# A mixture-of-experts stage: the overfull experts' branch at the end of the first group, the groups of four in second and fifth place, expert numbers read between transfers, and the embedding product in the second group

## The chip, the cores and the metric

The kernel runs on one core of a Trainium2 chip. A core has five engines that run side by side: TensorE (PE, with its weight loads listed as PEld), VectorE (DVE), ScalarE (ACT), GpSimd (POOL) and SyncE (SP), which here only issues transfers. Each engine works through its own list of instructions in order and waits on semaphores for the others. The metric is the device time of one execution in microseconds (us).

## The reference, cut to what matters

Two transformer blocks run one after the other on 512 tokens of width 1024. The first has a mixer and then a mixture of 32 experts; the second has a mixer, a dense feed-forward layer and a gated addition of a per-token embedding. The two pieces that the change touches are these:

```python
# first block: each token takes 2 of 32 experts (one group of 8 is chosen first)
def expert_block(args):
    xb, e = args
    hid = jax.nn.silu(xb @ w_gate[e]) * (xb @ w_up[e])   # 1024 -> 512, twice
    return hid @ w_down[e]                               # 512 -> 1024
y = jnp.sum(y_buf[dest].reshape(T, TOP_K, D) * weights[..., None], axis=1)
x = x + y

# second block, its last line
h = h + gate * (p @ w_ple)          # p: 512 x 256, w_ple: 256 x 1024, not dependent on h
```

All weights are float32. One expert has 3 matrices of 2 MiB, so the 32 experts are 192 MiB, which the kernel reads once.

## The kernel before, in words

The mixer of the first block runs up to about 340 us of the profile. Then comes the stage of the experts, from about 340 to 862 us, and then the second block.

**Sets and groups.** The router's result is counted on the chip, and the experts are sorted by the number of their tokens into 32 positions; the first 4 positions are fixed experts (0 to 3), so that their weights can be loaded before the routing is known. Positions 0 to 15 are taken in pairs (sets 0 to 7, 64 token slots for each expert), positions 16 to 31 in fours (sets 8 to 11, 32 slots for each). A set is thus always 128 token rows. Two sets are a group, and `GROUPS` gives the order of the six groups. For each group `dispatch` gathers the rows of its 256 slots by 64 matmuls of a one-hot matrix with the tokens (L765), and `expert_rows` then does each set: gate and up product (L841), silu and product, transposes (L852), down product (L859), and the weighted scatter back into the tokens by matmuls (L866, L867) that VectorE adds to `x1` (L869). TensorE's time for a set is the same for a pair and for a four, since two or four experts share the array side by side; the weights are 12 MiB for a pair and 24 MiB for a four.

**Transfers.** The weights come in 192 chunks of 1 MiB (L616, SyncE's queue), in the order in which sets use them: per set gate, up and down, each in two halves. `load_chunks` gives a chunk the next free slot. There are 15 slots at first; two of them (13 and 14) are given to other tiles after their first use, so 13 go round. At each half matrix, the slots of the halves before are given back and the next chunks are asked for; on the chip SyncE waits, chunk by chunk, until TensorE has read the chunk that was in the slot. `cap` limits how far the chunks run ahead of set `S_PLE`: to 9 chunks of it. `chunk_ap` makes the address; for positions 4 and up it needs the expert's number, which SyncE reads from the sorted list with `value_load` (L598).

**The embedding product.** `ple_units` multiplies `p` by `w_ple` (split in high and low parts, 8 output tiles of 6 matmuls, L99). It takes 4 slots out of the ring (`lent`): two for its operands, two for its results, and its pieces are put between the pieces of the experts' work by `fill_in`. What is left of it runs in the second block (`for _ in fill[0]: pass`). Each half of the result (1 MiB) is written to DRAM (L1214).

**The branch.** An expert with more tokens than slots needs further passes. `overflow` counts them, every engine reads the count from SBUF (L962), and a branch (L963) jumps over a loop of such passes when there are none, as with these inputs. No instruction is moved across the branch on any engine.

**The order.** The framework's scheduler orders each engine's instructions ahead of time, by its own estimate of when operands are there, and may put a later group's gathering between an earlier set's products where no branch is in between. TensorE then runs that list strictly in order.

Of the kernel before, what the change touches and what calls it, by code (L numbers as in the profile page):

```python
# [2 lines left out]

# [25 lines left out]
def hybrid_moe_block(ctx: ExitStack, tc: tile.TileContext, A, out):  # L29
    nc = tc.nc  # L30
# [16 lines left out]
    def slot(i, dt=F32):  # L47
        if i >= 13:
            return mp.tile([128, 2048], dt, name=f"slot{i}", tag="zz" if i == 13 else "yy", bufs=1)
        if i >= NSLOT:  # L50
            return prt.tile([128, 2048], dt, name=f"slot{i}", tag=f"s{i}", bufs=1)
        return slots.tile([128, 2048 if 6 <= i < 10 else WB], dt, name=f"slot{i}", tag=f"s{i}")
# [5 lines left out]
    def bank(tag, shape=(128, 512)):  # L58
        return psp.tile(list(shape), F32, name=f"ps_{tag}", tag=tag, bufs=NPS[tag])
# [35 lines left out]
    def mm3(ps, lh, ll, rh, rl, first=True, last=True):  # L95

        seq = list(zip(lh, rh)) + list(zip(lh, rl)) + list(zip(ll, rh))
        for i, (a, b) in enumerate(seq):
            T.matmul(ps, a, b, start=first and i == 0, stop=last and i == len(seq) - 1)  # L99
# [471 lines left out]


    N_FIXED, N_PAIR = 4, 8
    GROUPS = ((0, 1), (8, 9), (2, 3), (4, 5), (6, 7), (10, 11))

    def positions(s):
        return range(2 * s, 2 * s + 2) if s < N_PAIR else range(4 * s - 16, 4 * s - 12)

    chunk_src, set_start = [], {}
    for s in [s for g in GROUPS for s in g]:  # L580
        set_start[s] = len(chunk_src)
# [2 lines left out]
                for p in positions(s):  # L584
                    chunk_src.append((m, kh, p))
    chunks = []
    S_PLE = GROUPS[-1][0]
    cap = [set_start[S_PLE] + len(RO) - 2 - 4]
    order = []
    expert_of = {}  # L590

    def chunk_ap(m, kh, p):
        ks = slice(4 * kh, 4 * kh + 4) if m < 2 else slice(2 * kh, 2 * kh + 2)
        src = (wg_d, wu_d, wd_d)[m]
        if p < N_FIXED:
            return src[p, :, ks, :]
        if p not in expert_of:
            expert_of[p] = nc.sync.value_load(order[0][0:1, p:p + 1], min_val=0, max_val=31)  # L598
        return src[bass.ds(expert_of[p], 1)].rearrange("e p k n -> p (e k) n")[:, ks, :]

    free = list(RO)
# [3 lines left out]
    def load_chunks(at):  # L605

        while ring_used[0] < at:
            i = held.pop(0)
            if i < 13:
                free.append(i)  # L610
            ring_used[0] += 1
        while free and len(chunks) < min(cap[0], len(chunk_src)):
            held.append(free.pop(0))
            m, kh, p = chunk_src[len(chunks)]
            c = slot(held[-1])[:, :2048].rearrange("p (k n) -> p k n", k=2 if m == 2 else 4)
            nc.sync.dma_start(c, chunk_ap(m, kh, p))  # L616
            chunks.append(c)


# [7 lines left out]
    def x_tile():  # L627
        return mp.tile([128, 2048], F32, name="xT", tag="xT", bufs=1)
# [35 lines left out]
    def one_hot(oh_, sl, t, n):  # L664

        o = oh_[:, t, :n]
        V.tensor_scalar(o, io256[:, :n], sl[:, t, 0:1], None, op0=ALU.is_equal)
        V.scalar_tensor_tensor(o, io256[:, :n], sl[:, t, 1:2], o.bitcast(F32), op0=ALU.is_equal, op1=ALU.add)

    def group_hot():  # L670
        return prt.tile([128, NT, 256], F32R, name="ohp", bufs=1)
# [124 lines left out]
    pres, lent = [], []  # L796

    def ple_units():
        cap[0] = len(chunk_src)
        lent.extend(free.pop(0) for _ in range(4))  # L800
        wv = slot(lent[0], F32R)[:, :4 * S].rearrange("p (i k n) -> p i k n", i=2, k=2)
        pT = slot(lent[1], F32R)[:, :4 * S].rearrange("p (i k s) -> p i k s", i=2, k=2)
        for k in range(2):
            pt = bank("pt", (128, 4, 128))
            for t in range(NT):
                T.transpose(pt[:, t], pin[:, t, k * 128:(k + 1) * 128], ident)
            ptf = pt.rearrange("p a b -> p (a b)")
            P.activation(pT[:, 0, k], ptf, AF.Copy)
            V.tensor_tensor(pT[:, 1, k], ptf, pT.bitcast(F32)[:, 0, k], op=ALU.subtract)
        for h in range(2):  # L810
            hs = slice(512 * h, 512 * h + 512)
            P.activation(wv[:, 0], praw[:, :, hs], AF.Copy)
            V.tensor_tensor(wv[:, 1], praw[:, :, hs], wv.bitcast(F32)[:, 0], op=ALU.subtract)
            i = lent[2 + h]
            pres.append((i, slot(i)[:, :4 * S].rearrange("p (t n) -> p t n", t=NT)))
            yield
            for t in range(NT):
                ts = slice(t * 128, (t + 1) * 128)
                ps = bank("mm")
                mm3(ps, [pT[:, 0, k, ts] for k in range(2)], [pT[:, 1, k, ts] for k in range(2)],  # L820
                    [wv[:, 0, k] for k in range(2)], [wv[:, 1, k] for k in range(2)])
                P.activation(pres[h][1][:, t], ps, AF.Copy, scale=0.5)
                yield

    fill = [iter(()), 0]

    def fill_in():
        if fill[1]:
            fill[1] -= 1
            next(fill[0])  # L830

    def expert_rows(xT, c0, n, hot, wsrc, w=64):

# [182 lines left out]

    for g, sets in enumerate(GROUPS):
        if g:
            oh_ = group_hot()
            sl = small.tile([128, NT, 2], F32, name="slp")  # L1020
            V.tensor_scalar(sl, slotn, -128.0 * sets[0], None, op0=ALU.add)
            for t in range(NT):
                one_hot(oh_, sl, t, 256)
            xT = dispatch(x_tile(), oh_, 256)
        else:
            oh_ = hot0
        for i, st in enumerate(sets):
            ps = positions(st)
            if st == S_PLE:
                load_chunks(set_start[st])  # L1030
                fill[:] = [ple_units(), 6]
                fill_in()

            def wsrc(m, half, e, k):
                c = set_start[st] + len(ps) * (2 * m + (half if m < 2 else k // 2))
                if e == 0 and k == 0 and (m < 2 or half == 0):
                    load_chunks(c)
                return chunks[c + e][:, k] if m < 2 else chunks[c + e][:, k % 2, 512 * half:512 * half + 512]

            def hot():  # L1040
                return turn_hot(oh_, 128 * i, 128), slot_weights(oh_, 128 * i, ps)

            expert_rows(xT, 128 * i, 128, hot, wsrc, 128 // len(ps))
        if g == 1:
            load_chunks(set_start[GROUPS[2][0]])
            overflow()

    es3.close()
    es_rt.close()
# [346 lines left out]
    order = [(0, 0), (0, 1), (0, 2), (1, 0), (0, 3), (1, 1), (1, 2), (1, 3)]  # L1396
# [41 lines left out]
```

## Time and profile before

| what | time |
|---|---|
| median of 3 runs | 1458.87 us (1453.91 to 1460.01) |
| the profiled execution's own time | 1456.99 us |
| its span, first to last instruction | 1455.2 us |
| TensorE busy | 1355.6 us (93%) |
| VectorE busy | 643.1 us (44%) |
| read from DRAM over the span | 279.56 MB |

The span is what the trace covers; the execution's own time has 1.8 us more around it. The busy share of TensorE is an average over stages with different limits: a record counts as busy while a matmul is in flight, and matmuls overlap, so a busy TensorE isn't one at its peak. In the stage of the experts the page's forty slices show both limits: a DMA row of 9 where transfers run without a gap, and PE digits of 6 to 8 at the same place where TensorE waits for them.

### The profile page before, as it was taken

The page shows a single profiled execution, that of the slowest core. Times are in us where ns is not written, and L with a number is a line of the kernel's source. Part 1 is how long each engine was busy: PE and PEld are TensorE (multiplying, and loading weights), DVE is VectorE, ACT ScalarE, POOL GpSimd, SP SyncE. Part 2 cuts the span into 40 slices and gives each one's busy share as a digit, 9 for nine tenths or more (in the row PEclk, how much of TensorE's full clock was granted, in tenths as well). Part 3 has the DMA queues.
Part 4 walks back from the last instruction along what each step waited for, and adds up shares of the span by engine and source line. Part 5 has one row for each costly group of instructions (what it writes and reads, how often), then busy time and mean ns, then how long its engine had stood idle before and what let it go on. Part 6 is the DMA issues. An engine that isn't in the chain of part 4 may idle for free.

```text
span 1455.2 us, 20277 instructions
## 1 busy us (share of the span) xinstructions
PE 1355.6 (93%) x8033; PEld 975.7 (67%) x8033; DVE 643.1 (44%) x1625; ACT 420.3 (29%) x805; POOL 82.5 (6%) x83
## 2 busy tenths in 40 slices
PE   8999999998998689999997789899999999999998
PEld 7888888884342143534342138677988998889988
DVE  7784548765321023222221134666844224442374
ACT  5455535363110011111021023433433113331231
POOL 3120200011000000000000000211000000000110
PEclk8999999999999999999999889999999999999999
DMA  5201322675789997999949983114233222332321
GB/s 178 89 30 59 80 80 67 239 281 207 304 344 419 420 385 289 419 420 409 374 175 421 401 304 113 34 41 134 87 100 102 88 88 87 100 103 88 116 106 55
DMA packets 105857, 285.11 MB, mean 196 GB/s; under 512 B 6052, under 2 KB 74234, under 8 KB 81183
## 3 DMA queue, kind: packets, MB, share of 16 engines
q1 hardware_dynamic: 101132, 272.85, 49.9%
q10 hardware_dynamic: 3506, 7.09, 1.3%
q0 software_dynamic: 1120, 3.84, 0.7%
q8 instruction: 64, 1.05, 0.3%
q14 instruction: 35, 0.28, 0.1%
HBM read 279.56 MB, written 4.20 MB: 195 GB/s over the span
## 4 chain that ended last, share of the span: by engine, by line
PE 53%; DMA 5%; DVE 4%; ACT 1%; issue 1%; POOL 0%; SPq 0%; DVEq 0%; ACTq 0%
PE ps_mm L99 27%; PE ps_mm L841 8%; PE ps_sc L99 6%; PE ps_mm L859 4%; PE ps_pt L765 2%; DMA slot<-in_w_down_dram 2%; DMA slot<-in_w_up_dram 2%; PE ps_sc L866 1%; PE ps_sc L867 1%; DMA slot<-in_w_gate_dram 1%; DVE slot L89 1%; PE ps_pt L180 1%; PE ps_po L1145 0%; DMA row<-in_b_ple_gate_dram 0%; PE ps_sc L1105 0%
## 5 line engine op out<-in xcount | busy, mean ns | idle before, releaser
L841 PE MATMUL ps_mm<-slot,xT 128*64 128x512 f32 (+1 forms) x1024 | 207.0, 616 | 28.8 <-DMA slot<-in_w_up_dram 22.1
L89 DVE TENSOR_TENSOR slot<-slot,slot 128x1024 fp32r<-128x1024 f32 (+2 forms) x114 | 137.9, 1226 | 142.4 <-ACT slot L88 82.8
L88 ACT ACTIVATE slot<-slot 128x1024 fp32r<-128x1024 f32 (+2 forms) x126 | 126.0, 1038 | 175.0 <-PE ps_sc L99 105.6
L99 PE MATMUL ps_mm<-slot,slot 128*128 128x256 f32 (+1 forms) x1024 | 173.1, 320 | 0.9 <-DVE slot L89 0.8
L841 PEld LDWEIGHTS ps_mm<-slot,xT 128*64 128x64 f32 (+1 forms) x1024 | 55.9, 126 | 156.4 <-issue 103.2
L99 PEld LDWEIGHTS ps_mm<-slot,slot 128*128 128x128 f32 x1024 | 144.3, 191 | 18.9 <-issue 5.2
L99 PE MATMUL ps_mm<-h_h,slot 128*128 128x512 f32 (+1 forms) x640 | 152.7, 387 | 0.0
L859 PE MATMUL ps_mm<-slot,zz 128*64 128x512 f32 (+1 forms) x512 | 130.8, 605 | 11.7 <-DMA slot<-in_w_down_dram 8.8
L99 PEld LDWEIGHTS ps_mm<-h_h,slot 128*128 128x128 f32 x640 | 116.5, 189 | 27.6 <-issue 1.8
L99 PE MATMUL ps_mm<-slot,hTh 128*128 128x256 f32 (+1 forms) x640 | 93.7, 293 | 0.6 <-ACT hTh L182 0.6
L849 DVE TENSOR_TENSOR zz<-zz,ps_mm 128x512 f32<-128x512 f32 x12 | 8.3, 688 | 185.1 <-PE ps_mm L841 185.1
L859 PEld LDWEIGHTS ps_mm<-slot,zz 128*64 128x64 f32 (+1 forms) x512 | 32.6, 123 | 84.8 <-issue 54.2
L99 PEld LDWEIGHTS ps_mm<-slot,hTh 128*128 128x128 f32 x640 | 83.2, 193 | 2.6 <-ACT hTh L182 1.2
L869 DVE TENSOR_TENSOR x<-ps_sc,x 128x512 f32<-128x512 f32 x96 | 62.4, 687 | 39.3 <-PE ps_sc L867 39.2
L99 PE MATMUL ps_mm<-h_l,slot 128*128 128x512 f32 (+1 forms) x320 | 77.9, 385 | 0.0
L99 PEld LDWEIGHTS ps_mm<-h_l,slot 128*128 128x128 f32 x320 | 58.4, 188 | 13.2
L863 DVE SCALAR_TENSOR_TENSOR yy<-ps_mm,ws,yy 128x512 fp32r<-128x512 f32 x24 | 18.0, 748 | 110.9 <-ACT yy L862 110.9
L99 PE MATMUL ps_sc<-slot,slot 128*128 128x256 f32 x448 | 57.5, 283 | 0.0
L862 ACT ACTIVATE yy<-ps_mm,ws 128x512 fp32r<-128x512 f32 x24 | 16.5, 688 | 140.1 <-PE ps_mm L859 140.1
L99 PEld LDWEIGHTS ps_sc<-slot,slot 128*128 128x128 f32 x448 | 55.3, 191 | 0.0
L866 PE MATMUL ps_sc<-yy 128*128 128x512 f32 x96 | 40.9, 455 | 8.7 <-DVE x L869 5.5
L99 PE MATMUL ps_mm<-slot,hTl 128*128 128x256 f32 (+1 forms) x320 | 48.0, 290 | 0.0
(366 smaller groups left out, 1915.9 us busy)
## 6 DMA issues: line engine op xcount, KB each, us to landing
slot<-in_w_gate_dram SPq DMA_DIRECT2D x64, 1024.0 KB
slot<-in_w_up_dram SPq DMA_DIRECT2D x64, 1024.0 KB
slot<-in_w_down_dram SPq DMA_DIRECT2D x64, 1024.0 KB
slot<-in_w_ff_dram SPq DMA_DIRECT2D x32, 1024.0 KB
slot<-in_w_in_dram SPq DMA_DIRECT2D x12, 1024.0 KB
slot<-in_w_in_dram SPq DMA_DIRECT2D x12, 512.0 KB
slot<-in_w_out_dram SPq DMA_DIRECT2D x8, 512.0 KB
slot<-in_w_ple_gate_dram SPq DMA_DIRECT2D x4, 1024.0 KB
```

The source lines that it names most:

```text
L88: P.activation(h_, r_, AF.Copy)
L89: (eng or V).tensor_tensor(l_, r_, h_.bitcast(F32), op=ALU.subtract)
L99: T.matmul(ps, a, b, start=first and i == 0, stop=last and i == len(seq) - 1)
L180: T.transpose(pt[:, c], src[:, (j + c) * 128:(j + c + 1) * 128], ident)
L765: T.matmul(ps[:, c], hh[:, t, ds_], oh_[:, t, :n], start=i == 0 and t == 0 and (c == 0 or not by_tile), stop=i == 1 and t == NT - 1, skip_ ...
L841: T.matmul(ps[w * e:w * e + w], xT[:, 4 * kh + k, c0 + w * e:c0 + w * e + w], wsrc(m, kh, e, k), start=kh == 0 and k == 0, stop=kh == 1 an ...
L859: T.matmul(ps[w * e:w * e + w], hT[:, k, w * e:w * e + w], wsrc(2, nh, e, k), start=k == 0, stop=k == 3, skip_group_check=True)
L862: P.activation(yh[:n], ps[:n], AF.Copy, scale=ws[:n])
L863: V.scalar_tensor_tensor(yl[:n], ps[:n], ws[:n], yh.bitcast(F32)[:n], op0=ALU.mult, op1=ALU.subtract)
L866: T.matmul(pc, oT[:n, t], yh[:n], start=True, stop=False)
L867: T.matmul(pc, oT[:n, t], yl[:n], start=False, stop=True)
L869: V.tensor_tensor(xs, pc, xs, op=ALU.add)
```

## The change

Five edits, all in the stage of the experts. The two groups at the end change places, so that the groups of four stand second and fifth. `overflow` is called at the end of the first group and not of the second. `S_PLE` is the first set of the second group and not of the last, so the embedding product runs there; `fill_in` is called 8 times for it and not 6, each call takes two output tiles, and two of its four slots go back to the ring when it is done. And a `value_load` is tied behind the transfer issued before it (`tc.issue_after`), except for the first after the branch's call. Line numbers of the changed file are 3 to 7 higher in this stage (L765 is L768, L841 is L847, L859 is L865, L866 and L867 are L872 and L873, L616 is L619, L598 is L600, L963 is L969).

```diff
-    GROUPS = ((0, 1), (8, 9), (2, 3), (4, 5), (6, 7), (10, 11))
+    GROUPS = ((0, 1), (8, 9), (2, 3), (4, 5), (10, 11), (6, 7))
...
-    S_PLE = GROUPS[-1][0]
+    S_PLE = GROUPS[1][0]
     cap = [set_start[S_PLE] + len(RO) - 2 - 4]
     order = []
     expert_of = {}
+    last_load = []
...
         if p not in expert_of:
-            expert_of[p] = nc.sync.value_load(order[0][0:1, p:p + 1], min_val=0, max_val=31)
+            with tc.issue_after(last_load[0]) if last_load else nullcontext():
+                expert_of[p] = nc.sync.value_load(order[0][0:1, p:p + 1], min_val=0, max_val=31)
...
-            nc.sync.dma_start(c, chunk_ap(m, kh, p))
+            src = chunk_ap(m, kh, p)
+            last_load[:] = [nc.sync.dma_start(c, src).ins]
...
                 P.activation(pres[h][1][:, t], ps, AF.Copy, scale=0.5)
-                yield
+                if t % 2:
+                    yield
+        free.extend(lent[:2])
+        del lent[:2]
...
             fill[1] -= 1
-            next(fill[0])
+            next(fill[0], None)
...
-                fill[:] = [ple_units(), 6]
+                fill[:] = [ple_units(), 8]
...
-        if g == 1:
-            load_chunks(set_start[GROUPS[2][0]])
+        if g == 0:
+            load_chunks(set_start[GROUPS[1][0]])
             overflow()
+            last_load.clear()
```

What this does to the engines' lists is shown at three places. A row is a source line, an operation, and its output and input tiles by name; x2 is two in a row.

SyncE's list before, at the branch's end: the untaken loop's last rows, and the first two rows of a run of 17 reads of expert numbers (`zz` holds the sorted list) that stands between the branch and the next transfer.

```order
L988 REGISTER_ALU
L988 COMPARE_AND_BRANCH
L988 UNCONDITIONAL_BRANCH
L963 UNCONDITIONAL_BRANCH
L962 ISA x2
L598 TENSOR_LOAD zz
L598 ISA x2
```

SyncE's list of the changed kernel at the same place: after the branch the next transfer (chunk 33, an up half of set 8) follows at once; each later number is read just ahead of the first transfer that needs it.

```order
L994 REGISTER_ALU
L994 COMPARE_AND_BRANCH
L994 UNCONDITIONAL_BRANCH
L969 UNCONDITIONAL_BRANCH
L619 ISA
L619 DMA slot_4905<-in_w_up_dram 128x2048
```

TensorE's list of the changed kernel at the end of the second group, where the branch stood before: matmuls of set 9's down product (by its slots) with the gathering of the third group (`ohp` is the one-hot matrix, `h2h` and `h2l` the tokens' high and low parts).

```order
L768 MATMUL ps_pt<-ohp,h2h 128x256
L865 MATMUL ps_mm<-slot_5267,zz 32x512 x2
L768 MATMUL ps_pt<-ohp,h2l 128x256
L768 MATMUL ps_pt<-ohp,h2h 128x256
L768 MATMUL ps_pt<-ohp,h2l 128x256
```

Before, none of those gathering matmuls stands ahead of the branch there. At the end of the first group it is now the other way round: the changed list has the scatter of set 1, the branch, then all 64 gathering matmuls of the second group in one piece, then the embedding product's transposes (`pin` is `p`) and set 8's first gate product.

```order
L768 MATMUL ps_pt<-ohp,h2l 128x256
L809 MATMUL ps_pt<-ident,pin 128x128 x4
L847 MATMUL ps_mm<-slot_4315,xT 32x512
L809 MATMUL ps_pt<-ident,pin 128x128 x4
L847 MATMUL ps_mm<-slot_4334,xT 32x512
```

In the second block, TensorE's list before has the embedding product's last 24 matmuls between the transposes of the keys and the query projection (`h_h`).

```order
L1207 MATMUL ps_pt<-ident,kk 128x128 x3
L99 MATMUL ps_mm<-slot_6613,slot_6614 128x512 x5
L1207 MATMUL ps_pt<-ident,kk 128x128
L99 MATMUL ps_mm<-slot_6613,slot_6614 128x512 x19
L99 MATMUL ps_mm<-h_h,slot_7369 128x512 x8
```

In the changed list those 24 matmuls are gone from there; they stand in set 8 and set 9 with the others of the product.

## Rows read from the trace of the kernel before

**Rows 1.** The page: the span.
```profile
span 1455.2 us, 20277 instructions
```

**Rows 2.** Windows by group: span, busy us of PE, PEld, DVE, ACT, POOL; PEclk, DMA share, GB/s.
```profile
417.20:523.30 106.10, 82.47 (x437) 23.34 (x436) 15.41 (x27) 6.33 (x10) 0.00 (x0) 1.00 0.97 399
...
535.85:603.40 67.55, 65.66 (x319) 29.64 (x318) 19.75 (x38) 8.02 (x14) 0.00 (x0) 1.00 0.81 331
603.40:673.00 69.60, 67.12 (x319) 30.51 (x320) 19.10 (x38) 8.01 (x14) 0.00 (x0) 1.00 1.01 420
673.00:745.40 72.40, 69.04 (x317) 31.25 (x318) 21.27 (x42) 9.08 (x15) 0.00 (x0) 1.00 0.77 315
745.40:861.70 116.30, 93.01 (x448) 25.80 (x447) 11.99 (x18) 10.18 (x16) 1.69 (x7) 0.94 0.94 379
```

**Rows 3.** TensorE's longest wait, 535.9 to 745 us, then 417 to 524: total, times, longest.
```profile
PE ps_pt L852 <- DVE zz L849: 2.9, 4, 0.9
...
PE ps_mm L841 <- DMA slot<-in_w_up_dram: 10.4, 7, 1.9
```

**Rows 4.** Timeline, first group's end (start, duration, engine, line): SyncE's issues and TensorE.
```profile
403.64 0.33 SPq L616 DMA_DIRECT2D slot<-in_w_up_dram  x1
...
412.18 0.40 PE L867 MATMUL ps_sc<-yy 128*128 128x512 f32 x1
...
417.21 7.93 PE L841 MATMUL ps_mm<-slot,xT 128*32 128x512 f32 x70
...
420.87 0.33 SPq L616 DMA_DIRECT2D slot<-in_w_up_dram  x1
```

**Rows 5.** Second group's end: TensorE's timeline, the branch's line by engine, SyncE, the window.
```profile
511.98 2.76 PE L859 MATMUL ps_mm<-slot,zz 128*32 128x512 f32 x14 [0.59 <-DMA slot<-in_w_down_dram]
...
522.59 0.40 PE L867 MATMUL ps_sc<-yy 128*128 128x512 f32 x1
...
525.59 0.55 PE L765 MATMUL ps_pt<-ohp,h2h 128*128 128x256 f32 x1 [2.60 <-DVE ohp L668]
...
535.85 13.95 PE L841 MATMUL ps_mm<-slot,xT 128*64 128x512 f32 x64
...
L963 DVEq COMPARE_BRANCH  x1: 76/76/76, 523.7 to 523.7; - x1
L963 DVEq EVENT_SEMAPHORE  x1: 21/21/21, 524.3 to 524.3; - x1
...
L963 SPq EVENT_SEMAPHORE  x9: 17/17/17, 525.7 to 545.0; - x9
...
555.54 0.35 SPq L616 DMA_DIRECT2D slot<-in_w_gate_dram  x1
...
523.30:535.85 12.55, 10.26 (x64) 10.05 (x64) 3.83 (x10) 1.68 (x4) 0.00 (x0) 0.73 1.01 414
```

**Rows 6.** The line that reads expert numbers, whole kernel: ns min/median/max, first and last start.
```profile
L598 SPq TENSOR_LOAD <-zz x28: 262/264/481, 360.8 to 554.8; - x28
```

**Rows 7.** Timeline of the last group: its start, its first transfer, its end.
```profile
744.83 0.60 PE L806 MATMUL ps_pt<-ident,pin 128*128 128x128 f32 x4
745.37 1.05 PE L841 MATMUL ps_mm<-slot,xT 128*32 128x512 f32 x2
...
752.05 0.33 SPq L616 DMA_DIRECT2D slot<-in_w_up_dram  x1
...
857.26 2.76 PE L859 MATMUL ps_mm<-slot,zz 128*32 128x512 f32 x14 [0.66 <-DMA slot<-in_w_down_dram]
...
860.61 1.06 PE L859 MATMUL ps_mm<-slot,zz 128*32 128x512 f32 x6
```

**Rows 8.** Timeline of TensorE, the third group's last down product.
```profile
592.65 1.93 PE L859 MATMUL ps_mm<-slot,zz 128*64 128x512 f32 x6
```

**Rows 9.** Timeline of TensorE in the second block: the embedding product's rest, the query projection.
```profile
885.57 1.41 PE L99 MATMUL ps_mm<-slot,slot 128*128 128x512 f32 x5
...
891.36 2.03 PE L99 MATMUL ps_mm<-h_h,slot 128*128 128x512 f32 x8
```

More of the change, by code (lines that the diff above doesn't have):

```diff
@@ L1 @@
 import math
-from contextlib import ExitStack
+from contextlib import ExitStack, nullcontext
 import concourse.bass as bass
```

## The prediction

> **What bounds the kernel now.** I read the page first: a span of 1455.2 us [rows 1] inside an execution of 1456.99 us, so 1.8 us lie around it. Then I cut the stage of the experts into its groups with the windows by stage [rows 2], because its two kinds of set have different limits. The third, fourth and last-but-one groups are pairs: 67.55, 69.60 and 72.40 us, of which TensorE is busy for 65.66, 67.12 and 69.04. The second and the last are fours: 106.10 and 116.30 us, TensorE busy for 82.47 and 93.01, with a DMA share of 0.97 and 0.94. Pairs are bound by TensorE, fours by transfers. The waits say the same: from the third group to the last-but-one TensorE's longest total wait is 2.9 us for VectorE, and none of that list's five rows is for a transfer; in the second group the longest is 10.4 us for one [rows 3]. At full flow the chip moves 420 GB/s (fourth group) [rows 2], so a chunk of 1 MiB takes 1,048,576 / 420,000 = 2.50 us, a four-set's 24 chunks 60 us, a pair set's 12 chunks 30 us.
>
> This gives the rule for what follows. In a pair group only TensorE's work counts. In a group of fours only this counts: when the first slot comes free, how many chunks are already there, and whether transfers then run without a gap. A slot that TensorE could have emptied earlier is lost only there.
>
> **Part 1, the start of the second group (later).** Before, the gathering of the second group was woven into set 1's scatter: the last scatter matmul ends at 412.58, set 8's first product starts at 417.21, and its first quarter (4 chunks) is read at 420.87, when SyncE's waiting transfer goes out [rows 4]. With the branch there, the gathering comes after it. The branch costs this, where it stands now: from the last scatter matmul's end (522.99) to the first gate product (535.85) are 12.86 us, of which 2.60 are a wait for VectorE's one-hot and the rest 64 gathering matmuls, at a granted clock of 0.73 on average [rows 5]. So the first product starts at 412.58 + 12.86 = 425.4. Two blocks of the embedding's transposes stand in it, 0.60 each [rows 7], then the quarter of 3.66 us as before: 430.3, that is **+9.4 us**. A part of the gathering ran at 1.2 GHz, after the idle 2.60 us; at the full 2.4 GHz its 10.26 busy us would be 10.26 x 0.73 = 7.5 and the term 6.6. I take 9.4, as the row of the branch itself has it; upward it could be 11.2, if the quarter takes what it took in the last group with the product's pieces in it (745.37 to 752.05, 6.7 us [rows 7]).
>
> SyncE stops at the branch too: nine waits from 525.7 to 545.0, until its 8 outstanding chunks have landed (8 x 2.50 = 20 us), and then 17 reads of numbers, until 555.54 [rows 5, 6]. In the new place this is free: the last chunk ahead of the branch is number 32 (cap of 9), issued before 403.64 (number 33 before [rows 4]), so the eight have landed by 424 at the latest, and SyncE's next transfer can't go before 430.3. The wait of 30 us at the old place goes, but I count nothing for it: behind it come pairs, and TensorE waited for no transfer there [rows 3].
>
> **Part 2, the second group's transfers (later).** Before, 13 chunks of set 8 (24 to 36) were there or on their way; 37 to 71 remained, and 35 chunks went from 420.87 to TensorE's start on the last one at 511.98: 91.1 us = 35 x 2.50 + 3.6. Now the cap lets 9 in, and 4 slots are lent to the embedding: 39 chunks remain, **+10.0 us**. And the embedding's two results, 1 MiB each, are written in this group, in the middle of the flow: 2 x 2.50 = **+5.0** (one of them was written in the last group before; bounds 0, if writes fit beside reads, and 5). TensorE takes the last chunk at 511.98 + 9.4 + 10.0 + 5.0 = 536.4. TensorE's 24 + 24 matmuls of the product fit in its idle 24 us of this group [rows 2] and cost nothing. If the ring of 9 or 11 slots left gaps in the flow, that would be added; see the rivals.
>
> **Part 3, from the second to the third group (earlier).** Before, from TensorE's last chunk (511.98) to the third group's first product (535.85) went 23.9 us: the down product's end, scatter, branch, gathering [rows 5]. Now the gathering stands between down products that wait for chunks. But the next set's chunks are not there: gate and up of set 2 need 8 transfers, the eighth lands 20 us after the last one of set 9, and the final quarter of the product takes 3.5; a product that ran unhindered for 13.95 us [rows 5] would end then if it started 9.5 us after that chunk. So 9.5 stand in the place of 23.9: **-14.4 us**. The scatter that stands between (its list is the same) fits in those 9.5. The third group starts, in effect, at 535.85 + 24.4 - 14.4 = 545.9.
>
> **Part 4, third and fourth group (same).** Both pairs, TensorE's work, 535.85 to 673.0, unchanged. The ring has 11 slots and not 13; TensorE needs 2 chunks at a time there, so I count nothing.
>
> **Part 5, fours fifth, pairs last (earlier).** Before, from 673.0: pairs 72.4 us, then from 745.4 fours until the last chunk (857.26) 111.9, then 4.4 to the last down product's end (860.61 + 1.06 = 861.67) [rows 2, 7]; in sum 188.7. Now fours first: as the second group before, from first product to last chunk 511.98 - 417.21 = 94.8, with 11 chunks there and not 13, so 94.8 + 5.0 = 99.8. The 12 us less than the old last group are its slots: it had 9 chunks, its first slot came free after 6.7 us and not 3.7, and it had an embedding write in it. Then 9.5 as in part 3, and a pair group with nothing to gather behind it: the third group's first product to its last down product, 592.65 + 1.93 - 535.85 = 58.7 [rows 5, 8], less 6 gathering matmuls that stood in it, 57.7. In sum 167.0: **-21.7 us**. This is the main gain: each gathering and 11 prefetched chunks are covered by the other resource.
>
> **Part 6, the second block (earlier).** The embedding's last 24 matmuls go: 885.57 to 891.36, on TensorE with nothing else running there [rows 9]: **-5.8 us**. Behind them stands a query projection whose split weights must be there; if VectorE were late with them, as little as 2 would be left. The end of the experts' stage (scatter, transposes, the key projection's weights) has the same order as before.
>
> **Sum.** +24.4 - 14.4 - 21.7 - 5.8 = -17.5: 1456.99 - 17.5 = 1439.5, say **1440 us**. The profiled execution is 1.9 us below the median of the runs, so against the median it is a gain of some 18 us, 1.3%. With the bounds above, the forecast's own range is 1432 to 1449.
>
> A rule that speaks against part 1: the Trainium skill's page "Runtime: NRT & Kernel Launch" (Instruction fetch mechanics) says that a taken branch to a place outside the small window of fetched instructions waits for a DMA to bring that page, and that run-time control flow is dear for this reason. Here the trace disagrees for the branch in its old place: VectorE's branch at 523.7 is followed by its next instruction at 524.3, 0.6 us [rows 5], and that is inside my 12.86. By the rule, with a fetch of 3.6 us (what part 2's first chunk took beyond its flow), the result would be 1443.
>
> **Rivals.**
> *The short ring starves the fours (slower).* With 9 slots and 4 chunks under TensorE, 5 are on their way, 12.5 us of flow; the down product holds 8 until its second half. If each of the second group's ten quarters left the flow dry for the 3.6 us that a first chunk takes beyond its own 2.50, it costs 36 us: 1476. It decides once the group's 41 MiB with the writes take 17.5 us more than 102, that is below about 360 GB/s. Against it: the last group ran with the same 9 slots and has a share of 0.94, including its slow start [rows 2].
> *The gathering isn't hidden (no change).* If TensorE's fixed order makes it wait for chunks and gather afterwards, twice some 7.5 us come back: 1455. For it: the order is made ahead of time from estimates. Against: the pair groups' gathering is woven in with 2 to 3 us of idle.
> *More than forecast (faster).* The clock stays whole at the branch (-2.8) and the writes fit beside the reads (-5.0): 1432, or less, if the third and last groups' products don't wait for chunks as in part 3.
> *A stall at the branch (faster, less).* If an engine finds nothing to run behind the jump in its new place and waits for its code for the 3.6 us of part 2's first chunk, the second group starts that much later: 1443. Against it: 0.6 us on VectorE in the old place [rows 5].
>
> **Numbers.** Forecast 0.55, starved ring 0.08, gathering not hidden 0.13, more 0.18, stall 0.06. A difference of 0.5%, 7.3 us, is about what a measurement of this kernel can tell from none; faster means below 1451.6. The first, fourth and fifth cases are faster but for a bit of the first: 0.77. Same: the third and that bit, 0.15. Slower 0.08. The range leaves out most of the starved ring and the far end of the fourth case: 1428 to 1457.
>
> **What would show it.** Set 8's first product near 425 us, the first transfer after the branch near 430; full flow (about 420 GB/s) from there to near 536 with no gap; gathering between down products at the end of the second and fifth groups; the third group's effective start near 546; the fifth group's last chunk near 783; the last down product near 850; no embedding matmuls after the keys' transposes. I am wrong if the flow has gaps in the second group, if pair groups wait for chunks beyond their first set, or if the fifth group takes as long as the old last one.

## The result, and the profile of the changed kernel

The changed kernel takes **1466.04 us** (median of 4 runs), the kernel before 1457.59 beside it: ratio 1.006, 95% interval 1.004 to 1.008. It is slower, and the forecast of 1440 us is 26 us off. Of the profiled execution the span is 1462.5 us, 7.3 more than [rows 1].

The windows of the changed kernel answer to [rows 2]. They are cut at the first product of the second group, its last chunk's landing, the end of set 2's gate and up product, the end of set 5's, the fifth group's first product, its last chunk's landing and the last down product (columns as in [rows 2]).

```profile
427.38:541.33 113.95, 95.25 (x508) 37.41 (x509) 16.22 (x37) 13.34 (x23) 0.16 (x2) 0.91 0.94 385
541.33:571.24 29.91, 28.43 (x126) 9.80 (x123) 7.26 (x12) 2.57 (x4) 0.00 (x0) 1.00 1.01 420
571.24:678.29 107.05, 99.93 (x440) 42.61 (x440) 30.55 (x63) 11.18 (x19) 0.00 (x0) 1.00 0.90 369
678.29:701.30 23.01, 22.23 (x118) 14.10 (x120) 7.34 (x12) 3.65 (x7) 0.00 (x0) 1.00 0.95 397
701.30:802.75 101.45, 82.44 (x446) 27.33 (x446) 13.09 (x27) 6.64 (x12) 0.11 (x1) 0.93 0.95 391
802.75:876.76 74.01, 68.63 (x290) 24.81 (x285) 16.05 (x24) 7.02 (x11) 1.48 (x4) 1.00 0.90 359
876.76:1462.50 585.74, 567.12 (x3619) 501.29 (x3618) 292.74 (x539) 189.50 (x310) 26.05 (x20) 0.99 0.29 90
```

The kernel before, cut at the same events (its last two groups as one stretch):

```profile
417.21:511.98 94.77, 73.01 (x402) 20.11 (x401) 9.26 (x17) 4.96 (x8) 0.00 (x0) 1.00 0.96 397
511.98:549.80 37.82, 33.66 (x165) 17.85 (x166) 10.67 (x20) 3.65 (x7) 0.00 (x0) 0.91 0.82 340
549.80:649.90 100.10, 96.51 (x453) 41.42 (x452) 30.76 (x63) 11.78 (x20) 0.00 (x0) 1.00 0.94 389
649.90:673.00 23.10, 22.32 (x118) 14.16 (x120) 7.39 (x12) 3.65 (x7) 0.00 (x0) 1.00 1.01 420
673.00:861.67 188.67, 162.02 (x763) 57.02 (x763) 33.26 (x59) 19.26 (x31) 1.69 (x7) 0.96 0.88 354
861.67:1455.20 593.53, 575.51 (x3642) 507.69 (x3642) 293.14 (x539) 191.69 (x314) 26.04 (x20) 0.99 0.29 91
```

| stretch | forecast | measured | miss |
|---|---|---|---|
| part 1, second group's first transfer | +9.4 | +10.8 | 1.4 |
| part 2, from there to its last chunk | +15.0 | +18.5 | 3.5 |
| part 3, to the end of set 2's product | -14.4 | -7.9 | 6.5 |
| part 4, set 2 to set 5, to the fifth group | 0 | +6.9 | 6.9 |
| part 5, fifth and sixth group (175.5 for 188.7) | -21.7 | -13.2 | 8.5 |
| part 6, the rest | -5.8 | -7.8 | -2.0 |
| sum | -17.5 | +7.3 | 24.8 |

Part 1's time is that of SyncE's first transfer after the branch, which is also where part 2 begins (420.87 before, [rows 4]):

```profile
431.71 5.15 SPq L619 DMA_DIRECT2D slot<-in_w_up_dram  x7
```

So every part but the first and the last is wrong by 3.5 to 8.5 us, all to the same side. Three views say where to look. SyncE's waits from 425 to 560 us (us in total, times, longest): its queue stands still for the embedding's own write, twice.

```profile
SPq L619 <- PE ps_mm L847: 51.8, 11, 23.5
SPq L619 <- PE ps_mm L865: 28.5, 7, 10.5
SPq L619 <- DMA ple<-slot: 24.7, 2, 12.9
```

TensorE's waits for chunks in the second group (427 to 557 us): nearly all stand in the gate and up product (L847), almost none in the down product (L865).

```profile
PE ps_mm L847 <- DMA slot<-in_w_up_dram: 12.9, 7, 3.8
...
PE ps_mm L865 <- DMA slot<-in_w_down_dram: 0.6, 1, 0.6
```

And the chain that ended last (start, duration, work): the write is on it, and so are three pieces of gathering between set 9's down products, which I had called covered.

```profile
489.44 15.90 DMA ple<-slot
...
530.50 3.05 PE ps_pt L768 x25
533.55 1.83 PE ps_mm L865 x4
535.39 3.26 PE ps_pt L768 x26
538.65 3.55 PE ps_mm L865 x20
542.20 1.02 PE ps_pt L768 x7
```

### The profile page after: what moved, and what is told of

Its sections match the earlier page's. It is cut to its first block, busy times and chain, and to the rows that moved or that the text cites. A ratio compares the mean times of both kernels' runs of the same rounds, so it can differ in the third digit from the quotient of the medians.

```text
span 1462.5 us, 20268 instructions
## 1 busy us (share of the span) xinstructions
PE 1360.6 (93%) x8033; PEld 976.8 (67%) x8033; DVE 645.4 (44%) x1625; ACT 420.1 (29%) x805; POOL 82.5 (6%) x83
## 4 chain that ended last, share of the span: by engine, by line
PE 55%; DMA 9%; DVE 5%; ACT 1%; issue 1%; POOL 0%; SPq 0%; DVEq 0%; ACTq 0%
PE ps_mm L99 26%; PE ps_mm L847 9%; PE ps_sc L99 6%; PE ps_mm L865 6%; DMA slot<-in_w_up_dram 4%; PE ps_pt L768 3%; DMA slot<-in_w_down_dram 2%; PE ps_sc L872 1%; PE ps_sc L873 1%; DMA slot<-in_w_gate_dram 1%; DMA ple<-slot 1%; DVE slot L89 1%; PE ps_pt L180 1%; DVE x L875 0%; PE ps_po L1152 0%
## 5 line engine op out<-in xcount | busy, mean ns | idle before, releaser
L847 PE MATMUL ps_mm<-slot,xT 128*64 128x512 f32 (+1 forms) x1024 | 218.2, 646 | 29.2 <-DMA slot<-in_w_up_dram 23.5
L847 PEld LDWEIGHTS ps_mm<-slot,xT 128*64 128x64 f32 (+1 forms) x1024 | 57.2, 130 | 166.5 <-issue 112.5
L865 PE MATMUL ps_mm<-slot,zz 128*64 128x512 f32 (+1 forms) x512 | 124.2, 611 | 5.9 <-ACT zz L860 3.0
L865 PEld LDWEIGHTS ps_mm<-slot,zz 128*64 128x64 f32 (+1 forms) x512 | 34.2, 125 | 66.7 <-issue 52.3
L99 PEld LDWEIGHTS ps_mm<-h_l,slot 128*128 128x128 f32 x320 | 58.5, 189 | 13.2
L872 PE MATMUL ps_sc<-yy 128*128 128x512 f32 x96 | 41.3, 454 | 10.0 <-DVE x L875 6.8
```

The lines of the kernel that those rows point to most:

```text
L847: T.matmul(ps[w * e:w * e + w], xT[:, 4 * kh + k, c0 + w * e:c0 + w * e + w], wsrc(m, kh, e, k), start=kh == 0 and k == 0, stop=kh == 1 an ...
L865: T.matmul(ps[w * e:w * e + w], hT[:, k, w * e:w * e + w], wsrc(2, nh, e, k), start=k == 0, stop=k == 3, skip_group_check=True)
L872: T.matmul(pc, oT[:n, t], yh[:n], start=True, stop=False)
```

## The experiments

Each ratio is to the kernel before, measured in turns on the same chip (its medians lay between 1457.3 and 1458.5 us). The runs stand in four batches on four chips (e1 to e4, e5 to e8, e9 to e12, e13 to e16), so the changed kernel's own 1466.04 is from another batch than the runs that are set against it.

| run | change | us | ratio (95%) |
|---|---|---|---|
| e1 | changed, all 4 slots back | 1460.68 | 1.0021 (1.0010 to 1.0031) |
| e2 | changed, embedding in the fifth group | 1460.29 | 1.0018 (1.0004 to 1.0032) |
| e3 | changed, fours last | 1469.92 | 1.0082 (1.0064 to 1.0099) |
| e4 | changed, branch at the second group's end | 1464.50 | 1.0057 (1.0035 to 1.0078) |
| e5 | changed, embedding behind the last set | 1448.39 | 0.9932 (0.9909 to 0.9955) |
| e6 | before, embedding behind the last set | 1444.70 | 0.9915 (0.9892 to 0.9938) |
| e7 | e6 and fours fifth | 1441.08 | 0.9873 (0.9850 to 0.9896) |
| e8 | before, branch first and reads between | 1466.29 | 1.0055 (1.0035 to 1.0074) |
| e9 | changed, last gathering a set earlier, results written as in e1 | 1462.42 | 1.0027 (1.0013 to 1.0041) |
| e10 | changed, products between scatter steps | 1464.40 | 1.0044 (1.0027 to 1.0062) |
| e11 | changed, embedding's writes last | 1457.17 | 0.9990 (0.9972 to 1.0007) |
| e12 | e7 with e10's order | 1437.60 | 0.9862 (0.9840 to 0.9884) |
| e13 | changed, a pair set's whole list by hand | 1455.66 | 0.9994 (0.9977 to 1.0011) |
| e14 | e7 with e13's list | 1438.40 | 0.9870 (0.9853 to 0.9887) |
| e15 | e5 with e13's list | 1441.48 | 0.9896 (0.9879 to 0.9913) |
| e16 | before, reads between transfers | 1457.73 | 0.9994 (0.9979 to 1.0008) |

**The embedding's place: e1, e2, e11, e5, e6.**

```diff
e1
-        free.extend(lent[:2])
-        del lent[:2]
+        free.extend(lent)      # each half written inside ple_units
+        lent.clear()
e2
-    S_PLE = GROUPS[1][0]
+    S_PLE = GROUPS[4][0]
e11
-        nc.scalar.dma_start(ple[h].rearrange("(t p) n -> p t n", p=128), v)
+        with tc.issue_after(last_load[0]):
+            nc.sync.dma_start(ple[h].rearrange("(t p) n -> p t n", p=128), v)
e5, e6
+    S_PLE, cap = None, [len(chunk_src)]
...
+    load_chunks(len(chunk_src))    # behind the loop over the groups
+    for _ in ple_units():
+        pass
```

> The changed kernel with all four of the embedding's slots given back (each half of the result is written as soon as it is done), so that 13 slots go round from set 9's second half on, and not 11. TensorE's list in the pair groups stays the same. Theory ORDER (the pair groups grew from 137 to 144 us because TensorE's list puts a set's whole scatter ahead of the next set's products): pair groups stay at 143 to 145 us, only the fifth group's first slots help, 2 x 2.5 us: 1460 to 1463. Theory RING (the pair groups are short of slots): pair groups back to 137, and the 5 us: 1452 to 1456.

With 13 slots the stretch from set 2's to set 5's product is the same 107 us, with the same 440 matmuls; only the fifth group is 5 us shorter (96.5 to its last chunk, 101.5 in the changed kernel). So the ring isn't what the pairs lost. Window of e1:

```profile
571.90:678.90 107.00, 99.92 (x440) 42.61 (x440) 30.57 (x63) 11.19 (x19) 0.00 (x0) 1.00 0.95 389
```

> The changed kernel with the embedding's product in the fifth group (fours) and not in the second: no cap, no lent slots and no write of 1 MiB in the second group; all of these in the fifth. Theory WRITE AND CAP: the second group's last chunk lands 10 + 5 + 2 us earlier, near 524, and the fifth group loses about as much: total 1463 to 1468. Theory RING: the third and fourth group have 13 slots, and are back at 137 us: 1456 to 1460. Theory ORDER: they stay at 144 us, total as by WRITE AND CAP.

Without the embedding the second group runs 94.9 us from first product to last chunk (94.8 before), with it 114.0: **19.1 us** for a product whose 48 matmuls are less than 12 us of TensorE (24 took 5.8, [rows 9]). In the fifth group of the profiled execution it costs 118.1 - 96.5 (e1) = 21.6. The pairs stay at 107.0. The total, 1460.3, lies above the range for RING and below that for the other two. Why it is below stays open: the execution that was profiled took 1466.1, 5.8 above the median, and no less than the changed kernel, so its trace can't show where the typical run is shorter.

```profile
429.00:523.90 94.90, 76.32 (x450) 27.46 (x453) 13.92 (x34) 6.65 (x12) 0.00 (x0) 0.96 0.96 396
685.90:804.00 118.10, 96.30 (x502) 36.34 (x501) 15.39 (x30) 13.46 (x23) 0.27 (x3) 0.91 0.91 371
```

> The changed kernel with the embedding's two writes on SyncE's queue behind the last weight transfer. Theory WRITE (in the second group the two writes take 5 us of flow and hold SyncE up for another 2 to 3): first product to last chunk 106 to 107 us and not 114, total 1457 to 1461. Rival (writes fit beside reads, the group's length is its uncovered chunks and its clock): 1464 to 1467.

The writes alone are 7.3 us of the 19: 106.7 us to the last chunk, and SyncE's waits for them are gone. The total is back at that of the kernel before.

The two waits didn't cost alike. In the changed kernel SyncE stood still for the first write until 461.0, and the flow went on at 421 to 428 GB/s (451 to 461 us), since transfers issued earlier were still running. The second wait, until 505.3, outlasted them, and the flow broke off (same columns as above):

```profile
501.00:506.00 5.00, 1.96 (x7) 0.28 (x4) 0.00 (x0) 0.60 (x1) 0.00 (x0) 1.00 0.59 242
506.00:511.00 5.00, 1.22 (x6) 0.20 (x8) 0.00 (x0) 0.00 (x0) 0.00 (x0) 0.66 0.91 323
```

Against 420 GB/s that is some 3 us of flow lost (an estimate from these two rows), about what the writes cost beyond the 5.0 of their bytes.

> The changed kernel with the embedding's product behind the last set: no cap and no lent slots in any group; it takes four slots that the last weights have left, and its 48 matmuls stand between the last down product, the scatter and the second block. Theory EMBEDDING (in a group of fours the product costs its 4 uncovered chunks, its two writes and what SyncE waits for them, some 19 us, and its matmuls cost less than that anywhere else): -19 in the second group, -5 in the fifth, +8 to +14 at the end: 1449 to 1458. Rival: it is a wash, as my prediction had it (part 2's 15 us against some 12 for the 48 matmuls): 1460 to 1464.

> The kernel before with nothing changed but the embedding's product, behind the last set as in the run above. Here the last set is a four and its down product waits for transfers, so part of the 48 matmuls stands in its gaps. Theory EMBEDDING: the last group falls from 111.8 us (first product to last chunk) to 95 to 97, and the end grows by 0 to 6: 1443 to 1449. Rival (the last group's length was its clock and its late first slot, not the cap): 1455 to 1460.

Both came as EMBEDDING said, e5 0.6 below its range: 17.6 us off the changed kernel, 13.8 off the kernel before. In e6 the last group's stretch to its last chunk is 95.0 us, where 111.9 stood before, at the same order of the groups:

```profile
745.00:840.00 95.00, 76.88 (x411) 22.72 (x410) 11.70 (x17) 8.29 (x13) 0.00 (x0) 0.96 0.96 393
```

**The groups' sequence: e3, e7.**

```diff
-    GROUPS = ((0, 1), (8, 9), (2, 3), (4, 5), (10, 11), (6, 7))
+    GROUPS = ((0, 1), (8, 9), (2, 3), (4, 5), (6, 7), (10, 11))
```

(e3 on the changed kernel; e7 the other way, on e6.)

> The changed kernel with the groups in the old sequence, (6, 7) fifth and (10, 11) last. If fours in fifth place are worth what the traces give (from the fifth group's first product to the last down product 175.5 us in the changed kernel, 188.7 before): 13 us slower, 1479. But 9 of those us were the old last group's cap and its embedding write, which this kernel doesn't have there: then 4 us slower, 1470. If the sequence is worth nothing: 1466.

> The run above with the fours in fifth and the pairs in last place. The branch stays at the second group's end. If the sequence itself is worth what the changed kernel and its variant with the fours last differ by (4 us): 1440 to 1446. If that difference is lost because the embedding's matmuls now stand beside a set that TensorE bounds (12 us uncovered, in place of 0 to 6): 1446 to 1454.

Fours in fifth place are worth 4 us in the one and 3.6 in the other, not 21.7. What I had booked to the sequence was mostly the cap and the write, which left the last group (16.9 us shorter without them and the product, e6) and came back in the second.

**The branch and TensorE's list: e4, e8, e10, e13, e16.**

> The changed kernel with the branch back at the second group's end. The second group then starts near 417 and not 427 (-10), the third group starts 24 us after the last chunk and not some 16 (+8), and its list has the products between the scatter's matmuls again: by theory ORDER the third group is 3 us shorter: 1459 to 1462. By my prediction's parts 1 and 3 (+9.4 and -14.4 for the move) it is 5 us slower than the changed kernel: 1471.

The result, 1464.5, lies between the two, and its trace holds something else: TensorE's branch took 6.2 us, and VectorE waited 5.5 us for it. In the seventeen other kernels here the same row shows 352 to 368 ns. The row of the branch's line for TensorE's queue (ns min/median/max, first and last start), then VectorE's first row behind it:

```profile
L969 PEldq COMPARE_BRANCH  x1: 6212/6212/6212, 544.6 to 544.6; - x1
```
```profile
550.97 0.62 DVE L670 TENSOR_SCALAR ohp<-io,slp 128x256 fp32r<-128x256 f32 x2 [5.52 <-PEq L969]
```

So this run can't say what the branch's place is worth. e8 can:

```diff
-        if g == 1:
-            load_chunks(set_start[GROUPS[2][0]])
+        if g == 0:
+            load_chunks(set_start[GROUPS[1][0]])
             overflow()
+            last_load.clear()
```

(with the reads tied as in the change; ring, embedding and sequence as before.)

> The kernel before with the branch at the first group's end and the numbers read between transfers, nothing else. In its TensorE list all pair sets have the scatter ahead of the next set's products, as in the changed kernel, though the ring has 13 slots and the embedding is in the last group. Theory ORDER: first product of the second group +10, from its last chunk to the third group's first product ended -8, third and fourth group 107 us between the ends of sets 2 and 5 and not 100: 1463 to 1468. Theory RING OR EMBEDDING (the list's form costs nothing by itself): 100 us there, 1457 to 1461.

> The kernel before with the expert numbers read between transfers and nothing else. Then the 17 reads behind the branch (some 10 us of SyncE) are gone. All theories: no wait of TensorE was for these, 1456 to 1460; its list has small differences in sets 6 and 7 (slot weights and scatter), which by theory LIST could cost up to 2 us.

The reads do nothing that can be told from zero (e16); the branch alone costs as much as the whole change (1.0055 and 1.006), whose other parts about cancel: the embedding's new place costs 3.9 (17.6 - 13.8, e5 and e6), the sequence wins about 4. In e8's trace stand +10.4 at the start, 31.4 us to set 2's product where 37.8 stood, and then 106.3 us where 100.1 stood, though ring and embedding are those of before:

```profile
554.10:660.40 106.30, 99.55 (x440) 42.76 (x440) 29.85 (x59) 11.18 (x19) 0.00 (x0) 1.00 0.95 389
```

My word ORDER for it was too narrow, as e10 shows:

```diff
+                    if m == 0 and (4 * kh + k) % 2 == 1 and late:
+                        with tc.issue_after(mi.ins):
+                            late.pop(0)()      # one step of the last set's scatter
```

> The changed kernel with TensorE's list put right by hand where a pair set follows: the four steps of the second half's scatter are each tied behind two more steps of the next set's gate product, so products stand between them. Nothing else changes; branch, embedding and ring stay. Theory ORDER: the ends of set 2's and set 5's products lie 100 to 103 us apart and not 107, the last pair group is 2 to 3 shorter, total 1456 to 1460. Rival (VectorE's additions or the chunks set the pace, not the list): 1464 to 1467.

Products now stand between the scatter's steps, and set 2 to set 5 takes 108.8 us; the total is in the rival's range. The scatter's second half isn't the place. The timelines of a set side by side show it. First the kernel before, from set 2's product to set 3's (TensorE: start, us, line, count, [idle before]):

```profile
550.15 0.59 PE L940 MATMUL ps_po<-wds,ohp 128*128 128x4 f32 x4
550.69 0.75 PE L852 MATMUL ps_pt<-ident,zz 128*128 128x128 f32 x4
551.27 0.60 PE L790 MATMUL ps_pt<-ident,ohp 128*128 128x128 f32 x4
551.63 0.59 PE L940 MATMUL ps_po<-wds,ohp 128*128 128x4 f32 x4
552.18 4.50 PE L859 MATMUL ps_mm<-slot,zz 128*64 128x512 f32 x18
556.68 0.73 PE L866 MATMUL ps_sc<-yy 128*128 128x512 f32 x2
557.34 1.08 PE L859 MATMUL ps_mm<-slot,zz 128*64 128x512 f32 x4
...
562.06 0.59 PE L841 MATMUL ps_mm<-slot,xT 128*64 128x512 f32 x1
```

Then the changed kernel at the same place:

```profile
571.98 0.75 PE L858 MATMUL ps_pt<-ident,zz 128*128 128x128 f32 x4 [0.85 <-DVE zz L855]
572.57 0.60 PE L793 MATMUL ps_pt<-ident,ohp 128*128 128x128 f32 x4
573.48 3.71 PE L865 MATMUL ps_mm<-slot,zz 128*64 128x512 f32 x16 [0.31 <-ACT zz L860]
577.11 0.61 PE L946 MATMUL ps_po<-wds,ohp 128*128 128x4 f32 x4
578.23 0.58 PE L946 MATMUL ps_po<-wds,ohp 128*128 128x4 f32 x4 [0.51 <-DVE ws L950]
578.74 3.65 PE L865 MATMUL ps_mm<-slot,zz 128*64 128x512 f32 x14
582.32 0.73 PE L872 MATMUL ps_sc<-yy 128*128 128x512 f32 x2
...
585.27 0.50 PE L872 MATMUL ps_sc<-yy 128*128 128x512 f32 x1 [0.55 <-DVE x L875]
...
585.93 0.64 PE L847 MATMUL ps_mm<-slot,xT 128*64 128x512 f32 x1
```

Before, the slot weights (L940) fill TensorE's wait for VectorE's product, and the first half's scatter stands between down products, so VectorE's additions run beside them: 9.9 us from the first down product to the next set's first product. In the changed list the weights (L946) stand inside the down product with a wait, the scatter behind nearly all of it with another: 12.45 us. e13 ties a pair set's whole list by hand in the sequence that the kernel before has there:

```diff
+                    if pair:
+                        after_pe(down)      # each tied behind the one before
+                        q += 1
+                        if steps and q in (1, 3, 5):
+                            for f in steps.pop(0):      # scatter of the first half
+                                after_pe(f)
...
+                with tc.issue_after(lastg[0]) if len(ps) == 2 and g else nullcontext():
+                    return (oT, *slot_weights(oh_, 128 * i, ps))
```

> The changed kernel with TensorE's whole list of a pair set tied by hand, in the sequence that the kernel before has: the slot weights in the shadow of VectorE's product, the first half's scatter between matmuls of the second half's down product, the second half's scatter between the next set's products. Theory LIST (what pair sets lost stands in the down product's stretch, 12.5 us in the changed kernel against 9.9 before: slot weights, their wait, the scatter's waits): set 2's product end to set 3's falls from 33.8 to 30.8 or 31.2, set 2 to set 5 from 107 to 100 to 102, the last pair group is 2 us shorter: 1457 to 1460. Rival (pairs are held by something the list doesn't show): 1463 to 1467.

10.4 us less than the changed kernel, 1.3 below LIST's range, and nothing was edited but TensorE's list. From the first down product to the next set's first product it is 9.9 us again (570.41 to 580.29). Set 2 to set 5, then its two intervals that hold a group's gathering, e13:

```profile
567.90:669.90 102.00, 98.93 (x438) 39.52 (x436) 26.81 (x49) 11.06 (x19) 0.00 (x0) 1.00 0.98 392
597.99:640.07 42.08, 40.28 (x189) 18.46 (x189) 11.68 (x23) 4.73 (x9) 0.00 (x0) 1.00 0.95 371
670.00:695.75 25.75, 23.96 (x120) 13.89 (x121) 10.40 (x22) 3.54 (x7) 0.00 (x0) 1.00 0.76 298
```

Taken apart, from the end of one set's gate and up product to the next one's (us):

| interval | before | changed | e13 |
|---|---|---|---|
| set 2 to set 3 | 30.81 | 33.86 | 29.96 |
| set 3 to set 4, with a gathering | 36.69 | 38.61 | 42.08 |
| set 4 to set 5 | 32.48 | 34.55 | 29.93 |
| set 5 to the next group's first product, with a gathering | 23.10 | 23.09 | 25.75 |
| sum | 123.08 | 130.11 | 127.72 |

The intervals without gathering, 5.1 of the 7.0 us that the change added here (6.9 by the cuts of the first table), come back whole and more. Those with a gathering get slower by the tied list, so that of the 7.0 only 2.4 are won back up to the next group; the 1.9 that the change added to set 3 to set 4 are not shown to be the list's. The rest of e13's 10.4 lies elsewhere (profiled executions): 2.1 ahead of the second group, in the first group's pairs, 1.0 from there to set 2's product, 2.7 from the fifth group's start to the last scatter, and 2.2 in the second block, which the edit doesn't touch and where the granted clock was 1.00 against 0.99.

**Gathering: e9.**

```diff
+            if g == 4 and i == 1:
+                ahead = gather(GROUPS[5], True)      # into the results' two slots
```

> The changed kernel with the last group's gathering one set earlier: its one-hot and its gathered rows go into the two slots that hold the embedding's results (written out by then, and not in the ring), so it stands in set 10's down product and not in set 11's. Theory GATHER (TensorE has no room for 64 gathering matmuls between set 11's last chunks and its down product, so they push its end by some 5 us): from the fifth group's last chunk to the last down product 68 to 69 us and not 73.5, total 1460 to 1462. Rival (they only move, and set 10's slots come free later): 1464 to 1467.

From the fifth group's last chunk (806.9) to the end of the last down product (874.7) went 67.8 us, 74.0 in the changed kernel. To the last scatter matmul the gain is 5.3, and the median is 3.6 lower, 0.4 above GATHER's range. Gathered rows (`x_tile`) have one buffer, which the set before reads until its last gate and up product. So gathering can't stand where TensorE waits for chunks of those; it stands in the down product, which has less room.

**Towards a better kernel: e12, e14, e15** (code as in e10 and e13).

> The kernel with the embedding behind the last set, the branch at the second group's end and the fours fifth (1441.1 us), with the list put right by hand as in the run with products between the scatter's steps. Theory ORDER: of its pair sets the last two and set 2 to 5 in part have the scatter ahead of the products: 2 to 5 us faster, 1436 to 1439. Rival: 1440 to 1442.

> The kernel with the embedding behind the last set, the branch at the second group's end and the fours fifth (1441.1 us), with the same list tied by hand. Theory LIST: its set 2 to 5 lie 99.7 us apart already, the last two pair sets 31.5 and could gain 1: 1436 to 1440. Rival: 1440 to 1443.

> The same with the branch at the first group's end and the numbers read between transfers, that is the changed kernel with both its costs taken out (embedding behind the last set, list by hand). With the embedding behind the last set and the scheduler's own list it took 1448.4. Theory LIST: 6 to 8 less, 1440 to 1443, and the branch's place is worth nothing either way. Rival: the branch at the first group's end costs by itself (10 us at the second group's start against 7 won at its end): 1444 to 1448.

e12 and e14 are the fastest, 1.3 to 1.4% below the kernel before; their intervals overlap, so the two lists can't be told apart there, and against e7 (0.9850 to 0.9896) the gain isn't settled: in the profiled executions e7 and e12 reach the keys' transposes at the same time (876.4), and the 3.6 us between them lie behind, where TensorE's list is the same and the granted clock was 0.99 in e7 and 1.00 in e12. e15 is the changed kernel with both costs out, by its ratio 5 us below e5 through the list alone. It is 3.1 above e14, with overlapping intervals: whether the branch's place costs anything once the list is tied stays open.

## Why the prediction was wrong, part by part

**Part 1** was near, +10.8 for +9.4. From the last scatter matmul to the first product went 12.6 us (414.72 to 427.30) for the 12.86 taken over, though at a granted clock of 0.87 and not 0.73. The excess is ahead of it: set 1's last scatter ended 2.1 later than before, and e13's list gave these 2.1 back, so it belongs to part 4's mistake.

**Part 2** had the right terms and one wrong size. The writes are 7.3 and not 5.0 (e11): the trace shows them on a completion semaphore (104) that SyncE's transfers use too, so its in-order queue waited until each write had landed, and the second time the flow broke off. What is left, 11.9 us over the old group (106.7 for 94.8), holds the ten us for 4 chunks; no run measured these alone, and about 2 stay unexplained. The greater mistake is that I took the term as the price of a move and not of a place. I priced the cap in the second group in part 2 and its absence from the last in part 5, and never put the product where there is no cap at all. That place is worth 14 to 18 us (e5, e6).

**Part 3**: "the gathering stands between down products that wait for chunks" is the failed step. TensorE waited for chunks in the gate and up product (12.9 us for up chunks), not there (0.6); 7.3 us of gathering are on the chain, where I had put nothing, and moving it was worth 6.2 to the last down product in the last group (e9). My rival "the gathering isn't hidden" named this mechanism and its price (7.5 each time); I gave it 0.13.

**Part 4**: "TensorE's work, unchanged" failed. The work is the same, its sequence isn't, because the list is made again when anything ahead of it moves. I had the changed list at hand and read it at a few places, none of them inside a pair set. e8 shows that moving the branch is enough to bring the slower stretch about (106.3 for 100.1), e13 that the list is the cause in the intervals without gathering, 5.1 of the 7.0 us; for the 1.9 with a gathering it is only likely. Why the scheduler's estimate turns there wasn't tested, and the branch isn't all that decides: with it back in its old place (e4) set 2 to set 3 takes 30.8 again, set 4 to set 5 still 34.6. The short ring, my slower rival, has no part in it (e1).

**Part 5**: the fifth group itself was well sized (101.5 for 99.8). What failed is the same step as in part 3: after its last chunk 74.0 us went and not 67.2 (9.5 + 57.7), of which e9 explains 6.2. And the gain wasn't what I called it: 12 of the 21.7 were the old last group's cap and write, which part 2 paid back. The sequence alone is worth about 4 (e3, e7).

**Part 6**: -7.8 for -5.8, the sign right; where the other 2 us come from no run shows.

The rule of the Trainium skill on taken branches (page "Runtime: NRT & Kernel Launch", Instruction fetch mechanics) I set aside for a row of 0.6 us on VectorE. In the changed kernel that held: TensorE's branch took 0.35 us. In e4 it took 6.2 us, more than the 3.6 that I gave the rule; that it was code being fetched no row of that run shows.

## What to carry to other kernels

Price a piece of work where it stands, with the slots, caps and writes it brings, before you price its move: in a stretch bound by transfers a product of 12 us cost 19 (e2). Where a scheduler makes the list, compare the whole list of each bounding engine in every kind of stage, since a change at one place can reorder stages far behind it. And "hidden in the idle time" needs the buffer that lets it stand there: look for the last reader of what it overwrites.

## What the runs showed of the hardware that I had not expected

- The same branch took 6.2 us on TensorE in one kernel (e4) and 0.35 to 0.37 in seventeen others, six of which have it at the same group's end.
- Two writes of 1 MiB issued by ScalarE kept SyncE's queue from issuing reads for 24.7 us in total. During the first wait the flow stayed at 421 to 428 GB/s; behind the second it fell to 242 and 323 GB/s in two stretches of 5 us. Without the two writes the group was 7.3 us shorter, where their bytes at 420 GB/s make 5.0.
